# A two-layer hybrid mixer on one core: S5's tables of the first layer issued ahead of its first modulation, and the low parts of the out-projection's weights all on VectorE

## The chip, the core and the metric

The kernel runs on one core of one Trainium2 chip. The metric is the device time of one execution in microseconds (us); a run's figure is the median of several executions. Engines are named as the profile names them: PE is TensorE's matmuls and PEld its weight loads, DVE is VectorE, ACT is ScalarE, POOL is GpSimd, and SP is SyncE, whose queue issues most of the DMAs. Instructions of one engine run in the order in which they stand in its stream; what is late holds up what stands behind it.

## The reference, cut to what matters

Two layers run over 1280 tokens: 256 of a context and 1024 of the sequence, each with 1024 channels. A layer normalises its input and modulates it with values computed from a conditioning vector, projects it into four branches (RWKV-7, S5, SSD, GLA), mixes in each branch along the tokens, and projects the joined result back.

```python
def mixer_layer(h, mod, p, grid, init, need_out):
    shift, scale, gate = jnp.split(mod, 3, axis=-1)
    hn = rmsnorm(h, p['norm_pre']) * (1.0 + scale) + shift
    proj = hn @ p['w_in']
    ...
    y = jnp.concatenate([y_rw, y_s5, y_ssd, y_gla], axis=-1).astype(h.dtype) @ p['w_out']
    return h + gate * rmsnorm(y, p['norm_post']), states
```

The modulation is `mod = silu(c) @ ada_w[l] + ada_b[l]`. The S5 branch is a linear recurrence with complex diagonal coefficients. They come from parameters alone: `lam_bar = exp(lam * dt)`, `b_bar = ((lam_bar - 1) / lam) * b`. Nothing in them depends on the input or on the modulation.

## The kernel before

**Arithmetic.** Big products are made in three passes with 32-bit numbers that are split in a high part (rounded to the type fp32r) and a low part (the remainder): high by high, low by high, high by low. So weights and inputs are split on the chip. `split` (L1543) loads a half tile of 128x512 into one of two stage buffers, copies it to the high part on ScalarE (L1551) and subtracts it to make the low part; the engine of that subtraction is its last argument, VectorE unless it says "p" for GpSimd. All two-operand elementwise instructions pass through the helper `tt` at L342, and all matmuls through L330, so rows are told apart by their tiles.

**Order.** The program is written down layer by layer, and a scheduler then orders the instructions of each engine: among those which it finds ready by its own model of time, the one written first goes first. Tiles come from pools with a fixed number of buffers, and an instruction which needs a buffer waits until one is free. Pool T (L296) has eight buffers of 1280 columns, H (L302) six.

**Start of the first layer**, in `project` (L1714). `load_par` and `ada_in` load the parameters and the conditioning vector. `ada(0, 0)` (L1468) makes shift and scale in four pieces; each takes eight weight loads of 256 KB through a ring of four buffers (tile i_o), matmuls into a pj bank, copies on ScalarE and VectorE (L1488), and two small sums into the tile md. `prenorm` (L1500) takes five blocks of 256 columns: two loads into T buffers (n_x), squares on ScalarE, sums of squares on TensorE, an inverse root by eleven small VectorE instructions (qnx, qny, qnt), the product with it on VectorE and GpSimd, the modulation on VectorE and ScalarE, the cast to hi (L1528) and the subtraction to lo, of which one half is on each of VectorE and GpSimd. The last step needs md of all pieces. After that `load_con(False)` loads constants, and the projections start with the tiles misc and gk; their weights have four buffers, so that TensorE gets no others until the input's last block has passed through these two.

**S5's tables**, `s5_prep` (L705). Two parameter loads go into T buffers; three T buffers (all called z) are held to the end of the step. A setup of many small VectorE instructions makes powers and phases. Then each of four quarters makes complex products, the real half on VectorE and the imaginary half on GpSimd (z_w, z_o, z_es, z_ec, with z_tm), transposes and multiplies on TensorE in the one PSUM tile pz, and stores the tables to DRAM from SP (L828, L878, L880); their H buffers come free when the stores have landed. `s5_quarter` reads the tables much later, in the RWKV stage. The tuple MO gives the order in which a layer writes down its steps: p is `s5_prep`, g the GLA branch, s the SSD branch, r RWKV's projections. Before the change, p comes first in both layers, behind the projections of misc and gk.

**The out-projection**, `out_proj` (L1647). It splits eight weight tiles o_w0 to o_w7 of two halves each; the low parts alternate between GpSimd (even tiles) and VectorE (odd tiles). Then it goes over blocks of 256 columns. For the first block TensorE takes the weight tiles as they come. Just ahead of it stands the end of the RWKV stage, whose last steps make r_yt on VectorE and GpSimd and store it from GpSimd's queue (yd, L1454).

Of the kernel before, what the change touches and what calls it, by code (L numbers as in the profile page):

```python
# [24 lines left out]
KD = D // 128  # L25
# [205 lines left out]
ORDER = (3, 2, 4, 1, 0)  # L231
SJ = (3,5,6,7,9,10,11)

MO = 'pgsr'

RL = ('sm rq re', 'sm re rq')
RLL = 'rl hp tp qp'
# [20 lines left out]
class K:  # L258
# [1388 lines left out]
    def out_proj(self, l, h, dst, hi=None, lo=None):  # L1647
# [3 lines left out]
                          **{n: "oy" for n in ("o_yh", "o_yl", "o_y")}, **{n: "oo" for n in ("o_o", "o_acc", "o_sq", "o_x")})  # L1651
        W = []
        for m in range(8):
            W.append([x.rearrange("p (k m) -> p k m", k=KD) for x in self.split("o_w", f"o_w{m}", [128, 1024], 1, self.A["wout"][l, m], "pv"[m % 2])])
        nb = 1 if hi else 2
        for b in (0, 2, 3, 1, 4) if hi else (2, 3, 1, 4):
            b0 = b * 256
# [8 lines left out]
            x = self.R("o_x", [128, KD, 256])  # L1666
# [47 lines left out]
    def project(self, l, hi, lo, h):  # L1714

        outs = l == 0
        t0 = 0 if outs else TC
        self.l, self.fd, self.lates = l, {}, []
        self.rm = self.dr.tile([10, 128, 12, 128], F32, name=f"rm{l}")
        with ExitStack() as es:  # L1720
            if l == 0:
                self.pools(es, NT_, NQ_, NH_, left=AL[0].split(), **PA)
            else:
                self.pools(es, NT_, NQ_, NH_, right=AL[1].split(), **PA)
            if l == 0:
                self.load_par(0)
                self.ada_in()
                for _ in self.ada(0, 0, "pj", ("i_o", 4)):
                    pass
                self.prenorm(h, hi, lo)  # L1730
                self.load_par(1)
                pieces = self.adas(0)
            else:
                pieces = iter(())
            self.load_con(False)
            small = self.S("omu", [128, 10])
            self.omu, self.kkh = small[:, 0:8], small[:, 8:10]
            self.ts(self.omu, self.p("mu", 0, 8), -1.0, 1.0, OP.mult, OP.add)
            self.ts(self.kkh, self.p("kk", 0, 2), 0.5, None, OP.mult, OP.bypass)

            def gla():
                if G1[l] == "misc gk":
                    self.proj("gq", hi, lo, t0)
                self.proj_tok("gv", hi, lo)
                self.proj_tok("gg", hi, lo, t0 // 128)
                self.gla(Lazy(self, t0), outs)

            def ssd():
                for n in ("sB", "sC", "sx0", "sx1"):
                    self.proj(n, hi, lo)  # L1750
                self.proj_tok("sz", hi, lo, t0 // 128)
                self.ssd(Lazy(self, t0), outs)

            def rw():
                for n in ("k0", "k1", "wl", "al", "r0", "r1", "v0", "v1"):
                    self.rw_proj(n, hi, lo, outs)
                    next(pieces, None)

            self.proj(G1[l], hi, lo, t0)
            for n in MO:  # L1760
                {"p": lambda: self.s5_prep(l), "g": gla, "s": ssd, "r": rw}[n]()
            for _ in pieces:
                pass
# [63 lines left out]
```

## Time and profile before

| what | us |
|---|---|
| median of 3 runs | 2244.4 |
| lowest and highest of them | 2242.67, 2246.63 |
| the profiled execution, its own time | 2243.13 |
| its span, first to last instruction | 2241.4 |
| PE, DVE, ACT, POOL busy in it | 1947.4, 1529.2, 916.7, 846.5 |

The profile is of one execution. "Busy" is the time in which an engine had an instruction of the kind in work; a matmul's end is modelled. A row of a timeline gives start, duration, engine, line, operation, what is written and read, and in brackets the engine's idle time just before it and what ended it.

### The profile page before, as it was taken

How to read it: one execution, taken by the hardware profiler on the slowest of the kernel's cores; microseconds unless marked ns; L12 is line 12 of the kernel's file. 1: busy time of each engine (PE TensorE's matmuls, PEld its weight loads, DVE VectorE, ACT ScalarE, POOL GpSimd, SP SyncE). 2: the span in 40 equal slices, each digit the busy share in tenths (PEclk: the TensorE clock that was granted, in tenths of full speed). 3: DMA queues.
4: the chain of work that ended last, by engine and by line, in shares of the span. 5: the costliest groups of instructions: out<-in, count | busy, mean ns of one | idle time of the engine just before them, and what ended most of it. 6: DMA issues, size and time to landing. Idle time of an engine off the chain costs nothing. (4 is left out here: it accounts for less than half of the span.)

```text
span 2241.4 us, 45148 instructions
## 1 busy us (share of the span) xinstructions
PE 1947.4 (87%) x17712; PEld 1664.7 (74%) x17712; DVE 1529.2 (68%) x3423; ACT 916.7 (41%) x2009; POOL 846.5 (38%) x965
## 2 busy tenths in 40 slices
PE   6777999999997887878799779999999787889697
PEld 4667889678886676765799667887888676676497
DVE  3877646794146888885377786677754899896344
ACT  2434314333256447632233544234335755544220
POOL 0446460342024455532322255522332454542222
PEclk9889999999998888979999899999999989889698
DMA  7234425434633222214333335242234232212332
GB/s 247 74 118 132 157 83 170 128 115 133 187 99 116 88 74 81 70 40 140 90 114 113 120 125 175 89 145 80 70 112 125 98 105 68 86 47 73 122 104 95
DMA packets 204021, 246.83 MB, mean 110 GB/s; under 512 B 28384, under 2 KB 145632, under 8 KB 203808
## 3 DMA queue, kind: packets, MB, share of 16 engines
q1 hardware_dynamic: 169936, 213.13, 30.6%
q10 hardware_dynamic: 33008, 28.45, 3.9%
q8 instruction: 139, 2.28, 0.4%
q0 software_dynamic: 864, 2.36, 0.3%
q14 instruction: 74, 0.61, 0.1%
HBM read 169.27 MB, written 76.71 MB: 110 GB/s over the span
## 5 line engine op out<-in xcount | busy, mean ns | idle before, releaser
L330 PE MATMUL pj<-hi,i_wh 128*128 128x512 f32 (+1 forms) x696 | 180.2, 379 | 18.3 <-DVE hi L1528 13.2
L330 PE MATMUL pj<-lo,i_wh 128*128 128x512 f32 (+1 forms) x696 | 176.9, 372 | 0.1
L330 PE MATMUL pj<-hi,i_wl 128*128 128x512 f32 (+1 forms) x696 | 174.3, 368 | 2.7 <-DVE i_wl L342 2.7
L342 DVE TENSOR_TENSOR i_wl<-i_w,i_wh 128x512 fp32r<-128x512 f32 x108 | 84.8, 791 | 107.6 <-ACT i_wh L1551 37.6
L330 PEld LDWEIGHTS pj<-hi,i_wh 128*128 128x128 f32 x696 | 124.2, 199 | 43.1 <-DVE hi L1528 13.4
L330 PEld LDWEIGHTS pj<-hi,i_wl 128*128 128x128 f32 x696 | 123.9, 195 | 25.6 <-DVE i_wl L342 3.2
L330 PEld LDWEIGHTS pj<-lo,i_wh 128*128 128x128 f32 x696 | 124.0, 197 | 22.6 <-issue 2.6
L330 PE MATMUL px<-r_UV,r_A 128*64 128x64 f32 x1216 | 108.2, 247 | 17.0 <-DVE r_UV L1379 9.8
L330 PEld LDWEIGHTS px<-r_UV,r_A 128*64 128x64 f32 x1216 | 92.6, 157 | 37.5 <-DVE r_UV L1379 13.9
L1551 ACT CAST i_wh<-i_w 128x512 fp32r<-128x512 f32 x108 | 66.0, 620 | 122.0 <-PE pj L330 80.8
L1289 DVE TENSOR_TENSOR r_X<-r_X,r_tp 128x30 f32<-128x30 f32 (+1 forms) x300 | 93.8, 313 | 8.0
L342 DVE TENSOR_TENSOR r_tp<-r_N,r_X 128x30 f32<-128x30 f32 (+1 forms) x300 | 90.5, 302 | 7.2
L330 PE MATMUL pb<-r_AD,r_BK 128*128 128x256 f32 x320 | 85.2, 407 | 5.5 <-POOL r_BK L342 3.6
L342 POOL TENSOR_TENSOR r_S<-r_S,r_PM 64x256 f32<-64x256 f32 x72 | 54.0, 750 | 79.0 <-DVE r_S L342 66.8
L342 DVE TENSOR_TENSOR r_A<-pb,rcon 128x512 f32<-128x512 f32 x80 | 53.5, 682 | 42.2 <-PE pb L330 41.9
L330 PEld LDWEIGHTS pb<-r_AD,r_BK 128*128 128x128 f32 x320 | 60.9, 201 | 17.1 <-POOL r_BK L342 3.9
L330 PE MATMUL pj<-i_wh,hi 128*128 128x256 f32 x448 | 71.0, 296 | 2.9 <-ACT i_wh L1551 1.5
L345 POOL TENSOR_SCALAR r_AD<-r_AR 64x512 f32<-64x512 f32 (+1 forms) x80 | 54.4, 680 | 48.9 <-PE pb L330 42.4
L330 PE MATMUL pu<-r_rs,r_TT 128*64 128x128 f32 x320 | 49.2, 303 | 21.1 <-ACT r_rs L1375 20.8
L342 POOL TENSOR_TENSOR o_o<-o_o,o_x 128x512 f32<-128x512 f32 x18 | 23.8, 1323 | 114.7 <-DVE o_o L348 113.5
L330 PE MATMUL pj<-i_wl,hi 128*128 128x256 f32 x448 | 66.8, 289 | 0.2 <-DVE i_wl L342 0.2
L330 PEld LDWEIGHTS pj<-i_wh,hi 128*128 128x128 f32 x448 | 61.4, 198 | 6.7 <-issue 2.7
(469 smaller groups left out, 5445.9 us busy)
## 6 DMA issues: line engine op xcount, KB each, us to landing
i_w<-in_win SPq DMA_DIRECT2D x108, 256.0 KB, 3.0
r_in<-rm SPq DMA_DIRECT2D x36, 512.0 KB, 4.5
a_w<-in_ada SPq DMA_DIRECT2D x64, 256.0 KB, 3.8
rm<-i_o SPq DMA_DIRECT2D x48, 256.0 KB, 2.5
o_y<-yd SPq DMA_DIRECT2D x36, 256.0 KB, 3.0
i_o<-in_ada SPq DMA_DIRECT2D x32, 256.0 KB, 4.6
z_st<-s5t SPq DMA_DIRECT2D x32, 256.0 KB, 2.7
o_w<-in_wout SPq DMA_DIRECT2D x32, 256.0 KB, 2.7
```

The source lines that it names most:

```text
L330: self.nc.tensor.matmul(out, lhsT, rhs, start=start, stop=stop, skip_group_check=True)
L342: (self.nc.vector if e == "v" else self.nc.gpsimd).tensor_tensor(out, a, b, op)
L345: (self.nc.vector if e == "v" else self.nc.gpsimd).tensor_scalar(out, a, s1, s2, op0, op1)
L1289: last = nc.vector.tensor_tensor(X[:, :, :i, r0:4], X[:, :, :i, r0:4], tmp[:, :, :i, r0:], OP.add)
L1551: self.nc.scalar.copy(hi[:, v], w)
```

## The change

`s5_prep` of the first layer, and `load_con(False)`, whose constants it uses, are written down ahead of `ada(0, 0)`; the second layer keeps its order. In `out_proj` the last argument of `split` is dropped, so that all low parts of the weights are made on VectorE. Nothing else differs; no arithmetic is added or left out.

```diff
-MO = 'pgsr'
+MO = ('gsr', 'pgsr')
...
-            W.append([x.rearrange("p (k m) -> p k m", k=KD) for x in self.split("o_w", f"o_w{m}", [128, 1024], 1, self.A["wout"][l, m], "pv"[m % 2])])
+            W.append([x.rearrange("p (k m) -> p k m", k=KD) for x in self.split("o_w", f"o_w{m}", [128, 1024], 1, self.A["wout"][l, m])])
...
             if l == 0:
                 self.load_par(0)
                 self.ada_in()
+                self.load_con(False)
+                self.s5_prep(l)
                 for _ in self.ada(0, 0, "pj", ("i_o", 4)):
                     pass
                 self.prenorm(h, hi, lo)
...
-            self.load_con(False)
+            if l:
+                self.load_con(False)
...
-            for n in MO:
+            for n in MO[l]:
                 {"p": lambda: self.s5_prep(l), "g": gla, "s": ssd, "r": rw}[n]()
```

## Rows read from the trace of the kernel before

**Rows 1.** The page, parts 1 and 2: busy time by engine; TensorE in 40 slices.

```profile
PE 1947.4 (87%) x17712; PEld 1664.7 (74%) x17712; DVE 1529.2 (68%) x3423; ACT 916.7 (41%) x2009; POOL 846.5 (38%) x965
...
PE   6777999999997887878799779999999787889697
```

**Rows 2.** Stretches: busy us (count) of PE, PEld, DVE, ACT, POOL; clock, DMA, GB/s.

```profile
0.00:74.50 74.50, 52.01 (x408) 38.38 (x409) 29.97 (x112) 24.94 (x51) 8.15 (x11) 1.00 0.69 220
74.50:130.00 55.50, 36.76 (x176) 30.52 (x174) 54.22 (x155) 17.60 (x35) 28.20 (x17) 0.75 0.11 38
130.00:250.00 120.00, 103.94 (x875) 93.62 (x875) 85.27 (x102) 57.45 (x102) 70.17 (x45) 0.94 0.45 148
250.00:400.00 150.00, 150.00 (x1502) 129.23 (x1492) 88.93 (x164) 46.81 (x102) 52.48 (x79) 0.99 0.41 130
```

**Rows 3.** Timeline, VectorE and GpSimd: start, duration, line, operation; last md, last lo.

```profile
74.57 0.15 DVE L348 SCALAR_TENSOR_TENSOR md<-md,par 128x4 f32<-128x4 f32 x1
...
125.57 2.53 POOL L342 TENSOR_TENSOR lo<-n_x,hi 128x1024 fp32r<-128x1024 f32 x1 [11.18 <-DVE hi L1528]
```

**Rows 4.** Instructions by tile, the tables': least, median, greatest ns; first and last start.

```profile
L342 DVE TENSOR_TENSOR z<-z x160: 109/176/2479, 68.5 to 1299.8; 128x16 f32<-128x16 f32 x96, 128x32 f32<-128x32 f32 x24, 128x64 f32<-128x64 f32 x24, 128x256 f32<-128x256 f32 x8
...
L342 POOL TENSOR_TENSOR z_w<-z x8: 1062/1426/2676, 91.5 to 1379.7; 128x512 f32<-128x512 f32 x8
L342 DVE TENSOR_TENSOR z_w<-z x8: 671/689/2041, 92.9 to 1380.5; 128x512 f32<-128x512 f32 x8
...
L342 POOL TENSOR_TENSOR z_es<-z x8: 1684/1741/2713, 136.4 to 1399.7; 128x640 f32<-128x640 f32 x8
```

**Rows 5.** Instructions by tile, the prenorm's.

```profile
L1528 DVE CAST hi<-n_x x10: 678/680/687, 47.9 to 124.8; 128x1024 fp32r<-128x1024 f32 x10
...
L342 DVE TENSOR_TENSOR lo<-n_x,hi x5: 1212/1216/1226, 49.2 to 123.5; 128x1024 fp32r<-128x1024 f32 x5
```

**Rows 6.** Timeline of VectorE and GpSimd: small operation alone, and beside lo.

```profile
32.78 0.16 DVE L342 TENSOR_TENSOR qnt<-qny 128x2 f32<-128x2 f32 x1
...
77.35 2.35 DVE L342 TENSOR_TENSOR qnt<-qny 128x2 f32<-128x2 f32 x1
...
76.97 8.15 POOL L342 TENSOR_TENSOR lo<-n_x,hi 128x1024 fp32r<-128x1024 f32 x3 [11.61 <-DVE hi L1528]
```

**Rows 7.** Timeline of GpSimd, second layer: first z_w, last z_es.

```profile
1271.37 1.89 POOL L342 TENSOR_TENSOR z_w<-z 128x512 f32<-128x512 f32 x1 [31.79 <-DVE z L342]
...
1405.45 2.03 POOL L342 TENSOR_TENSOR z_es<-z_es,z_tm 128x640 f32<-128x640 f32 x1
```

**Rows 8.** Waits of the SP queue, 75 to 250 us, then 0 to 75 us.

```profile
SPq L828 <- ACT z_wt L842: 33.9, 5, 26.6
...
SPq L828 <- DVE z_bp L857: 2.6, 1, 2.6
...
SPq L1482 <- PE pj L330: 20.7, 18, 6.4
```

**Rows 9.** Stretch 130 to 250 us, instructions on the tables' PSUM tile pz alone.

```profile
130.00:250.00 120.00, 10.52 (x208) 7.54 (x208) 3.55 (x16) 11.78 (x38) 0.94 0.45 148
```

**Rows 10.** Timelines of the first layer's end of RWKV: ScalarE, VectorE, GpSimd.

```profile
1051.96 1.14 ACT L1551 CAST o_w0h<-o_w 128x512 fp32r<-128x512 f32 x2
...
1067.73 0.88 DVE L348 SCALAR_TENSOR_TENSOR r_yt<-r_yt,par,r_ks 128x256 f32<-128x256 f32 x2
...
1068.74 1.26 POOL L342 TENSOR_TENSOR r_yt<-r_yt,r_fin 128x512 f32<-128x512 f32 x1 [8.09 <-DVE r_yt L348]
...
1071.79 2.50 POOL L342 TENSOR_TENSOR o_w0l<-o_w,o_w0h 128x512 fp32r<-128x512 f32 x2
```

**Rows 11.** Timeline of GpSimd, the second layer's.

```profile
2112.00 2.50 POOL L342 TENSOR_TENSOR o_w0l<-o_w,o_w0h 128x512 fp32r<-128x512 f32 x2
```

**Rows 12.** Instructions by tile, stage o_w.

```profile
L342 POOL TENSOR_TENSOR o_w2l<-o_w,o_w2h x4: 1277/1282/1291, 1080.4 to 2127.5; 128x512 fp32r<-128x512 f32 x4
L342 DVE TENSOR_TENSOR o_w3l<-o_w,o_w3h x4: 691/692/694, 1084.9 to 2132.4; 128x512 fp32r<-128x512 f32 x4
```

## The prediction

> **What bounds the kernel now.** I read the page first: TensorE is busy 87% of the span, and its line of 40 slices is 9 in long stretches and 6 to 8 at the start and in others [rows 1]. Where it says 9, only less matmul work could help; where it does not, TensorE waits, and a change can only shorten such waits. So I cut the first 400 us into stretches at two events [rows 2]: the last modulation value of the first layer (md, written at 74.57 us) and the last low part of the normed input (lo, ending at 128.1 us, called P below) [rows 3]. Up to 74.5 us TensorE waits for ada's weights, and VectorE is idle for 44.5 us of it. From there to P VectorE is busy 54.2 of 55.5 us: it is the bound, TensorE works 36.8 us at a granted clock of 0.75, between its two levels of 1.2 and 2.4 GHz. From 130 to 250 us TensorE leaves out 16 us at 0.94, and from 250 to 400 us it is full. Hence the S5 tables share VectorE with the prenorm before P, and disturb TensorE's feed until 250 us.
>
> **What the tables cost.** In the first layer they are 211 VectorE and 40 GpSimd instructions, of whose groups [rows 4] show the largest (counts there are for both layers). By the least durations, a quarter has on VectorE three z_w and three z_o at 0.67 us, three operations on 640 elements at 0.8 to 1.3 us and eleven small ones, about 9.1 us; on GpSimd six at 1.06 and 1.29 us and three at 1.6 to 1.7 us, 11.8 us. Four quarters: 83.6 us. The setup before them is some 130 VectorE instructions, mostly at 0.18 us, about 27 us with the larger ones. For the prenorm's five blocks of 256 columns and what else ran, summed in the same way over the instructions (lo at 1.21 us on VectorE and 2.5 us on GpSimd, the casts of hi at 0.68 us [rows 5]), about 34 us lie ahead of 74.5 us and 37 us behind.
>
> The two engines disturb each other: a 128x2 operation takes 0.16 us alone and 2.35 us while GpSimd runs the three lo subtractions [rows 6]. Between 74.5 us and P work of 68 us by least durations (37 prenorm, 31 tables) was done in 55.5 us, so the pair does **1.23 us of work in 1 us**. The Trainium skill, SBUF — State Buffer, section Who interferes with whom, says that this port pair is an exclusive lock for a VectorE instruction with two SBUF inputs against GpSimd's reads; the rows agree for the operation shown, not for all, since 1.23 is over 1. By that rule alone the tables' halves on the two engines would never overlap; this is the second rival below, with the rate 1.0.
>
> **Part 1, the tables ahead of ada.** The order is made by priority, so the tables now go first on every engine where they are ready.
> - Setup: the parameters land some 5 us into the run. 27 us of setup plus about 12 us of prenorm work on VectorE fill it until about 40 us; this was idle time, so it costs nothing. If ada's small copies and sums wait behind it, a few tenths each.
> - Quarters: in the second layer, where the tables stand ahead of nearly everything, GpSimd's first z_w starts at 1271.4 us and the last z_es ends at 1407.5 us [rows 7]: 34 us a quarter, longer than their 20.9 us of work, for they wait on buffers and stores. Starting at 35 us they end at about 171 us.
> - Ada: two more loads for constants and two for parameters stand ahead of its weights on SP, about 2 us, and I take 78 us for its end. Its later loads stand behind the tables' stores on SP, 70 issues a layer in all. SP waited in that way for 97 us between 75 and 250 us in eight groups, the longest shown, of which 26.6 us were one wait; the rest is 17.7 us a quarter. SP already waits 20.7 us for ada's ring in the first 75 us [rows 8]; the 1.25 quarters until 78 us bring 22 us, which I put beside it at no cost. If that cover is gone, ada is late: the third rival.
> - P: from 78 us the tables take 20.9/34 = 0.61 us per us of the pair's 1.23, the prenorm gets 0.62, and its 37 us take 60 us: 138 us. The tables hold three of the eight buffers in which the input is loaded, so its last blocks come about one block later; I add 5 us. **P moves from 128 to 143 us**, the wrong way. At rate 1.0 it would be 168 us (after ada the tables leave 0.39), at the 1.4 that I get from the same sum between 90 and 110 us, 130 us.
> - After P: from 130 to 250 us TensorE was busy 103.9 us, of which 10.5 us were the tables' own matmuls and transposes [rows 2, 9]. The other 93.4 us are 88 us at full clock. At P = 143 us 0.8 of a quarter is left, 17 us of work where 76 us were, so I keep 16 x 17/76 = 3.6 us of TensorE's idle time and 3 us for the rest. 143 + 88 + 6.6 = 238 us stands against 250 us: **12 us gained**. The bounds are P = 130 us, 24 us gained, and P = 168 us, where nothing of the tables is left: 168 + 88 = 256 us, 6 us lost.
> - The tables' activations and their three table loads on ScalarE, busy 25 of the first 74.5 us, cost nothing there. Their stores meet ada's loads, but the queues were busy 0.69 of that stretch and 0.11 of the next [rows 2]. Past 250 us TensorE is full, so what is gained by then should stay; that the GLA branch gets its buffers earlier is counted as nothing.
>
> **Part 2, the low parts on VectorE.** At the end of the first layer's RWKV part, ScalarE had the high part of the first weight tile at 1053.1 us, but GpSimd's subtraction runs at 1071.8 us: it stands in order behind the last r_yt and two DMA issues. VectorE is through with r_yt at 1068.6 us [rows 10]. The second layer shows the same, 2112.0 us [rows 11] with r_yt's sums ending 3.2 us earlier. Until then both stage buffers are full, and no further weight loads start. On VectorE the start comes 3.2 us earlier, the first tile is ready 0.6 us sooner (0.69 against 1.28 us [rows 12]), and three more even tiles save 0.6 us each in the chain of load, cast, subtraction: 3.2 + 0.6 + 1.8 = 5.6 us a layer, **11 us in all**, as TensorE waits for each tile in its first block and has the other blocks' work afterwards. VectorE takes on 16 subtractions in all, 11 us, in stretches where it waits for casts. Bounds: 1.5 us a layer, if TensorE can fill the gaps with the next block's tiles or SP is held by the loads of y; 18.7 us a layer, if the subtraction is put into VectorE's earlier gaps. I take 5.6 because GpSimd, idle before its last r_yt, did not get it there either.
>
> **The sum.** The profiled execution took 2243.1 us (span 2241.4 us), 1.3 us under the median of 2244.4 us. 2243.1 - 12 - 11 = 2220 us, and on the median's level **2221 us**.
>
> **The rivals.**
> 1. *The quarters fit.* If stores and buffers do not hold the quarters up while GpSimd is free, three are done by ada's end. With P at 130 us part 1 gives 24 us, and with part 2 up to 15 us: 2205 us. For it: GpSimd is busy only 8.15 us up to 74.5 us [rows 2]. Against: the 34 us a quarter.
> 2. *The two engines shut each other out.* P is 168 us, part 1 loses 6 us, part 2 gives 11 us: 2239 us. For it: the 2.35 us row. Against: the rate of 1.23.
> 3. *Ada's loads stand behind the stores on SP: slower.* If the 17.7 us a quarter fall on ada in full over 2.5 quarters, its end goes from 78 to 122 us. The prenorm then has 49 us beside the last quarters (30 us of work), 6 us alone, and its input, in five buffers, comes late as well, 6 us: P = 183 us, 183 + 88 = 271 us, 21 us lost. With 11 us from part 2 it is 10 us slower: 2254 us. It decides from an ada end of about 116 us. For it: one queue, in order, and the 26.6 us wait. Against: while the tables wait, ada's ready loads are meant to be put ahead of them.
> 4. *Little moves:* the order puts the tables where they were, or takes back later what is gained; 0 to 11 us from part 2 remain, 2240 us.
>
> **How the numbers follow.** About 0.2% (4.5 us) is what a measurement of this kernel can tell from no change. The forecast has 42%, rival 1 22%, rival 2 14% (half of it faster by more than that), rival 3 13%, rival 4 9% (5% of it faster). Faster: 42 + 22 + 7 + 5 = 76%; the same: 7 + 4 = 11%; slower: 13%. The range goes from 2196 us (rival 1 with the early subtraction in one layer) to 2250 us (rival 3 with P 4 us earlier).
>
> **What would show it.** The tables' setup must end near 40 us and their last store near 170 us; ada's last md should stand near 78 us, and P between 135 and 155 us; from P on TensorE should be at 9 tenths or more, and its full stretch begin some 12 us earlier relative to its work. In the out-projection, o_w0l must follow r_yt on VectorE at once, and the first block end 5 to 6 us sooner after it. An md later than 110 us, or P later than 175 us, makes the forecast wrong; so does a gain that is given back between 400 and 700 us, where VectorE is the busier engine.

## The result: 18 us slower, and the profile after

The changed kernel takes 2263.5 us (median of 6 runs, 2257.7 to 2268.5) against 2245.5 us for the kernel before on the same chip: a ratio of 1.0075, 95% interval 1.0057 to 1.0092. I had forecast 2221 us, and 2196 to 2250 us for the range. The sign was wrong.

The profiled execution of the changed kernel took 2268.5 us, with a span of 2266.7 us against 2241.4 us. It is the slowest of its six and the profile before is near the fastest, so the profiles lie 25.3 us apart where the medians lie 18.0. Read beside [rows 1], the slices of TensorE's busy share and clock, of the changed kernel, already show two places:

```profile
PE 1965.5 (87%) x17712; PEld 1683.7 (74%) x17712; DVE 1524.9 (67%) x3439; ACT 916.4 (40%) x2007; POOL 829.1 (37%) x949
...
PE   5689999999998877888799779989999777778697
...
PEclk8589999999997898888999889989999788889698
```

The first two slices are lower than before, and so are four of the five from the 33rd to the 37th (57 us each). The others differ by a digit or two here and there. To put sizes on this I took the same instruction in both traces as a milestone:

| milestone | before, us | after, us | difference |
|---|---|---|---|
| ada's last md of layer 0, end | 74.7 | 102.9 | +28.2 |
| last lo of the prenorm (P), end | 128.1 | 150.7 | +22.6 |
| a fifth of all projection matmuls done | 241.1 | 245.7 | +4.6 |
| RWKV stage of layer 0, first pu | 706.1 | 709.0 | +2.9 |
| the same stage, last pu | 1049.0 | 1062.7 | +13.7 |
| out-projection of layer 0, last matmul | 1213.2 | 1225.5 | +12.3 |
| RWKV stage of layer 1, first pu | 1762.1 | 1772.9 | +10.8 |
| the same stage, last pu | 2080.9 | 2110.5 | +29.6 |
| out-projection of layer 1, last matmul | 2224.7 | 2250.0 | +25.3 |

Read the steps between the lines. The front, where part 1 was made, ends 3 us late, which is not clear of the spread: in the seven kernels of this study that leave the front as it was, the first pu stands between 704.4 and 709.4 us. The two RWKV stages, which neither part edits, take 10.8 and 18.8 us longer. From the last pu to the last matmul of the out-projection, where part 2 was made, it takes 1.4 and 4.3 us less. Nearly all that was lost was lost where nothing was changed.

The front first: windows of the changed kernel (the columns of [rows 2]) and the timeline of md and of P, the answer to [rows 3].

```profile
0.00:74.50 74.50, 43.57 (x408) 32.62 (x410) 61.82 (x213) 27.29 (x59) 28.45 (x25) 0.79 0.69 217
74.50:130.00 55.50, 39.98 (x298) 32.95 (x288) 51.37 (x84) 20.08 (x50) 37.96 (x22) 0.70 0.41 129
130.00:250.00 120.00, 104.54 (x762) 92.06 (x761) 46.56 (x69) 48.94 (x76) 39.48 (x27) 0.91 0.41 138
250.00:400.00 150.00, 150.00 (x1476) 129.03 (x1474) 89.16 (x158) 45.26 (x93) 49.61 (x72) 0.99 0.34 108
```

```profile
102.73 0.16 DVE L348 SCALAR_TENSOR_TENSOR md<-md,par 128x4 f32<-128x4 f32 x1
...
148.22 2.51 POOL L342 TENSOR_TENSOR lo<-n_x,hi 128x1024 fp32r<-128x1024 f32 x1 [4.79 <-DVE hi L1528]
```

VectorE is filled from the start (61.8 us busy up to 74.5 us, where it had 30.0), as forecast, and GpSimd takes its share. But ada is 28 us late, and the granted clock of the first stretch falls from 1.00 to 0.79, between its two levels of 1.2 and 2.4 GHz, while TensorE, waiting more, is busy 43.6 us instead of 52.0.

The start of the out-projection in the changed kernel, the answer to [rows 10]:

```profile
1078.58 0.88 DVE L348 SCALAR_TENSOR_TENSOR r_yt<-r_yt,par,r_ks 128x256 f32<-128x256 f32 x2
1079.38 1.28 DVE L342 TENSOR_TENSOR o_w0l<-o_w,o_w0h 128x512 fp32r<-128x512 f32 x2
1079.59 2.21 POOL L342 TENSOR_TENSOR r_yt<-r_yt,r_fin 128x512 f32<-128x512 f32 x1 [7.27 <-DVE r_yt L348]
```

o_w0l now follows r_yt on VectorE at once, where it stood 3.2 us later on GpSimd.

Last the two RWKV stages as windows, from the first to the last pu (the matmul of the recurrent state), before and then after:

```profile
706.10:1049.00 342.90, 282.71 (x3473) 235.74 (x3472) 286.42 (x636) 179.74 (x431) 157.67 (x207) 0.88 0.27 82
1762.10:2080.90 318.80, 265.92 (x3364) 219.89 (x3364) 274.27 (x616) 173.07 (x420) 153.25 (x203) 0.91 0.26 80
```

```profile
709.00:1062.70 353.70, 289.88 (x3477) 240.10 (x3478) 283.72 (x636) 179.78 (x428) 164.54 (x207) 0.86 0.25 79
1772.90:2110.50 337.60, 271.00 (x3364) 227.69 (x3364) 271.83 (x615) 174.13 (x420) 151.40 (x203) 0.86 0.25 75
```

The numbers of instructions are the same (within a few at the edges of the windows), and VectorE and ScalarE work as long as before. What grew is TensorE's idle time (in layer 1 from 52.9 to 66.6 us) and, at a lower clock, its busy time. The same work, then, but in another order: on VectorE and ScalarE, the instructions of the two traces run in the same sequence for about two thirds of these stages in layer 0 and for a third in layer 1, while they agree to some 95% in the projections of the last 200 us ahead of the first stage. The program's planner writes the order down by its own estimate of when things are ready. That it had a different state to start from here is argued; the runs below show what a change of the order costs.

### The profile page after: what moved, and what is told of

It is laid out like the page before. It is cut to its first block, busy times and chain, and to the rows that moved or that the text cites. A ratio compares the mean times of both kernels' runs of the same rounds, so it can differ in the third digit from the quotient of the medians.

```text
span 2266.7 us, 45119 instructions
## 1 busy us (share of the span) xinstructions
PE 1965.5 (87%) x17712; PEld 1683.7 (74%) x17712; DVE 1524.9 (67%) x3439; ACT 916.4 (40%) x2007; POOL 829.1 (37%) x949
## 5 line engine op out<-in xcount | busy, mean ns | idle before, releaser
L342 DVE TENSOR_TENSOR i_wl<-i_w,i_wh 128x512 fp32r<-128x512 f32 x108 | 89.8, 836 | 153.2 <-PE pj L330 73.8
L330 PE MATMUL pb<-r_AD,r_BK 128*128 128x256 f32 x320 | 90.0, 426 | 4.6 <-POOL r_BK L342 2.1
L1289 DVE TENSOR_TENSOR r_X<-r_X,r_tp 128x30 f32<-128x30 f32 (+1 forms) x300 | 84.4, 281 | 7.6
L342 POOL TENSOR_TENSOR o_acc<-o_acc,o_sq 128x512 f32<-128x512 f32 x23 | 31.1, 1353 | 113.1 <-ACT o_sq L339 113.0
L330 PEld LDWEIGHTS pu<-r_rs,r_TT 128*64 128x64 f32 x320 | 41.6, 160 | 36.4 <-ACT r_rs L1375 32.7
L339 ACT ACTIVATE r_BK<-r_BK,r_PM 128x128 f32<-128x128 f32 x160 | 58.4, 396 | 21.8 <-PE pb L330 20.0
```

The lines of the kernel that those rows point to most:

```text
L330: self.nc.tensor.matmul(out, lhsT, rhs, start=start, stop=stop, skip_group_check=True)
L339: self.nc.scalar.activation(out=out, in_=in_, func=f, **kw)
L342: (self.nc.vector if e == "v" else self.nc.gpsimd).tensor_tensor(out, a, b, op)
L1289: last = nc.vector.tensor_tensor(X[:, :, :i, r0:4], X[:, :, :i, r0:4], tmp[:, :, :i, r0:], OP.add)
```

## The experiments

Two theories, and rivals. **A**: an edit anywhere makes the planner order the RWKV stages anew, and the order sets their length; the edits' own price is small. **B**: part 1's lateness at the front is handed down. **C**: part 2 overloads VectorE. **D**: the changed front leaves TensorE with a lower clock. All times are medians, each with its ratio to the kernel before on the same chip; the stages are from one profiled execution. Stage lengths are from first to last pu.

### The parts alone, and two controls

Part 1 alone (p1_tables) leaves out the second hunk of the change, part 2 alone (p2_lows) is that hunk only. The controls add one line to the kernel before, at its very start:

```
 null_v:
+        nc.vector.memset(self.cp.tile([128, 64], F32, name="nul"), 0.0)
 null_p:
+        nc.gpsimd.memset(self.cp.tile([128, 32], F32, name="nul"), 0.0)
```

> The tables ahead of ada alone; the out-projection's low parts as before (odd ones on GpSimd). Theory A (order): the front costs little, and the time is lost where an unedited stage gets another order. Then the last md of ada stands near 101 us and P near 151 us as in the changed kernel, the RWKV stage of layer 0 starts some 3 us late (before: 706 us) and gets 8 to 11 us longer than 343 us, the projections of layer 1 keep their length, and the RWKV stage of layer 1 (before: 319 us) comes out anywhere from 10 us shorter to 20 us longer, since its order differs from both kernels'. Rival B (own price): the late md and P are handed down, all of the +18 us of the changed kernel are there by 706 us, and part 1 alone is +18 to +25 us with both RWKV stages at their old lengths (within 3 us).

> The low parts of the out-projection's weights on VectorE alone; the tables where they were. Theory A (order): everything up to the end of the RWKV stage of layer 0 is as before within 1 us (1068.6 us for its last r_yt on VectorE); o_w0l starts 3 us earlier in both layers, the out-projections end 0 to 6 us earlier after it; the RWKV stage of layer 1, which has another order, changes its length by 3 us or more either way though nothing in it was edited. In sum -10 to +10 us. Rival C (VectorE overloaded): the 11 us of subtractions delay VectorE's chain in the out-projection, whose length grows by 3 us or more in each layer, with the RWKV stages unchanged.

> A control: the kernel before with one memset of an unused tile of 128x64 on VectorE at its very start, some 0.1 us of work, and nothing else. Theory A (order): the order of the instructions that the program's planner writes down reacts to so small a shift; one or both RWKV stages change length by 3 us or more, and the time leaves that of the kernel before by more than 0.2%, either way. Rivals B and C: the time stays within 0.2% and both stages keep their length within 2 us.

> A second control: the kernel before with one memset of an unused tile of 128x32 on GpSimd at its very start. Theory A: as in the first control, an RWKV stage changes by 3 us or more and the time by over 0.2%, not necessarily with the same sign as there; together with the first control and the two parts this gives the spread that an order alone makes. Rivals B and C: within 0.2%, stages within 2 us.

| kernel | time, us | ratio (95%) | stage of layer 0 | stage of layer 1 |
|---|---|---|---|---|
| p1_tables | 2284.4 | 1.0166 (1.0140 to 1.0191) | 355.1 | 344.2 |
| p2_lows | 2246.1 | 0.9994 (0.9978 to 1.0011) | 343.2 | 325.0 |
| null_v | 2245.5 | 0.9994 (0.9975 to 1.0012) | 341.2 | 326.7 |
| null_p | 2252.3 | 1.0022 (1.0002 to 1.0041) | 343.0 | 319.1 |

(Of the low parts it is the even ones that GpSimd makes before the change; the expectations of p1_tables and p1_late say odd.) Part 1 alone is slower than both parts together, by 21 us of medians. Its front is that of the changed kernel within 1.5 us, and the first pu of layer 0 stands at 708.9 us, 2.8 us late; so B, which wanted the whole loss there by 706 us, falls. Both stages are longer, as A expects, though both by more than its ranges (12 us where 8 to 11 stood, and 25 where up to 20 stood). Part 2 changes nothing in sum. The out-projections gain; the stage of layer 1, whose order it changes, took 325.0 us, 6 us more than before, but that lies within the spread of the controls below. Two later kernels with this same order, al_qp and a_q, took 328.0 and 326.9 us. Against C, no out-projection got longer: from VectorE's last r_yt to the last matmul they take 143.4 and 112.0 us, where it was 144.6 and 115.9.

The controls did not do what they were made for: the order of VectorE and ScalarE in their traces is that of before throughout, so the planner did not react, and the 0.2% of null_p, at the edge of its interval, are no effect of an order. So A's first half, that an edit anywhere makes a new order, is false as it stands. They tell something else: with one and the same order, the profiled stage of layer 1 comes out between 318.8 and 326.7 us, and that of layer 0 between 341.2 and 343.0 us. This is how far single executions lie apart.

### An order changed alone

If the order is the cause, it must be enough to change it in the kernel before. Memsets of a tile that is zero anyway, ahead of the RWKV stage, move the planner's estimate by a little. The first three edits and a fourth, of another kind:

```
 b_l1v2 (before), b_l0v12 (before), a_l0v12 (changed kernel), at the start of the RWKV part:
-        nc.gpsimd.memset(self.zero, 0.0)
+        nc.gpsimd.memset(self.zero, 0.0); [nc.vector.memset(self.zero, 0.0) for _ in range(2 if not outs else 0)]
 (b_l0v12 and a_l0v12: range(12 if outs else 0))
 a_late (changed kernel):
                 self.load_con(False)
-                self.s5_prep(l)
                 for _ in self.ada(0, 0, "pj", ("i_o", 4)):
                     pass
+                self.s5_prep(l)
                 self.prenorm(h, hi, lo)
```

> The kernel before with two memsets on VectorE (r_z, set to zero once more) at the start of the RWKV part of layer 1, well under 1 us of work, and neither part of the change. They tip the planner: the order of VectorE's and ScalarE's instructions in the RWKV stage of layer 1 becomes that of part 1 alone, instruction for instruction, while all before it stays as it was. Theory A (order): everything up to the first pu of layer 1 (1762 us) is as before, the stage from first to last pu takes about 344 us as in part 1 alone instead of 319 to 327, and the time rises by 17 to 25 us, to 2263 to 2271 us. Rivals B (own price of the edits, handed down) and D (a lower clock that the changed front leaves behind): nothing changed ahead, so the stage stays at 319 to 327 us and the time within 5 us of before.

> The kernel before with twelve such memsets on VectorE at the start of the RWKV part of layer 0, some 2 us of work, neither part of the change. The order in the RWKV stage of layer 0 becomes that of the changed kernel (98% of VectorE's and ScalarE's instructions in the same order), that of layer 1 becomes part 1's in full. Theory A: first to last pu of layer 0 353 to 357 us instead of 341 to 343, of layer 1 340 to 346 us instead of 319 to 327; with the memsets' 2 us the time is 2270 to 2285 us, part 1's own loss without part 1. Rivals B and D: at most the memsets' 2 us, 2246 to 2250 us.

> The changed kernel with the same twelve memsets at the start of the RWKV part of layer 0. Its order there stays nearly as it was (98%), but that of layer 1 becomes that of the kernel before, instruction for instruction. Theory A: the RWKV stage of layer 0 keeps its 354 to 356 us, that of layer 1 goes from 338 us back to 319 to 327; the time falls by 10 to 17 us, to 2246 to 2253 us. Rivals B and D: layer 1 keeps its 338 us, and the time goes up by the memsets' 2 us to about 2265 us.

> The changed kernel with the tables' call behind ada's first part instead of ahead of it, and still ahead of the prenorm; part 2 as in the change. In both RWKV stages the order is that of the kernel before, instruction for instruction. Theory A: first to last pu 341 to 345 us in layer 0, 319 to 327 in layer 1; ada's md is back near 75 us, P between 145 and 170 us, the start of the RWKV stage of layer 0 within 6 us of 706; with part 2's 1 and 4 us the time comes out at 2236 to 2250 us. Rival B: tables beside the prenorm cost the same or more, 2262 us or later, already there at the start of the RWKV stage of layer 0. Rival D: the stages stay near 354 and 338 us whatever their order, as long as the front is changed.

| kernel | time, us | ratio (95%) | stage of layer 0 | stage of layer 1 |
|---|---|---|---|---|
| b_l1v2 | 2273.1 | 1.0120 (1.0095 to 1.0146) | 341.8 | 340.5 |
| b_l0v12 | 2249.0 | 1.0008 (0.9993 to 1.0023) | 340.5 | 323.5 |
| a_l0v12 | 2267.3 | 1.0093 (1.0075 to 1.0111) | 355.2 | 336.9 |
| a_late | 2225.0 | 0.9895 (0.9861 to 0.9928) | 339.7 | 320.6 |

**b_l1v2** is the decisive one. It contains neither part of the change, and its milestones stand within 2.1 us of before's up to the end of layer 0's out-projection. Two memsets make it 25 us slower: 14 to 22 in the RWKV stage of layer 1, against the controls' 318.8 to 326.7 us, and some 5 in the projections ahead of it, where the order changed in places too (450 us from the out-projection's end to their own, where it was 443 to 446 in the order of before). Its expectation had the stage right (about 344 us), but not these 5 us, and the time lies 2 us above its range. TensorE's longest waits in that stage (total us, times, longest), of the kernel before:

```profile
PE pu L330 <- ACT r_rs L1375: 10.7, 8, 3.1
PE p L330 <- DVE z_x L342: 7.3, 3, 3.4
PE pi L330 <- ACT r_Rb L1324: 4.5, 5, 1.3
```

The stage's window in b_l1v2, and then the same waits there:

```profile
1770.30:2110.80 340.50, 275.83 (x3364) 229.78 (x3364) 275.77 (x615) 173.41 (x418) 153.64 (x203) 0.85 0.24 74
```

```profile
PE pu L330 <- ACT r_rs L1375: 25.1, 12, 6.2
PE p L330 <- DMA z_st<-s5t: 4.2, 2, 2.9
PE px L330 <- DVE r_UV L1379: 4.1, 2, 3.4
PE pi L330 <- DVE r_DN L1309: 4.1, 2, 3.0
```

The counts are the same, 3364 matmuls each, and VectorE's work is 274.3 and 275.8 us. But in the new order the state's matmul pu waits 25.1 us for ScalarE's r_rs, where it waited 10.7 us, and the waits on r_UV and r_DN are longer (1.2 and 0.8 us before). Here is the longest wait, of 6.2 us, in rows of VectorE, ScalarE and TensorE:

```profile
1819.59 0.41 DVE L1374 COPY r_rs<-px 64x256 f32<-64x256 f32 x1
1817.57 0.63 ACT L339 ACTIVATE r_th<-ps,r_sc 128x128 f32<-128x128 f32 x2 [3.71 <-POOL r_ks L345]
1821.17 0.63 ACT L339 ACTIVATE r_a<-ps,r_sc 128x128 f32<-128x128 f32 x2 [2.98 <-POOL r_BK L342]
1821.83 0.36 ACT L1375 COPY r_rs<-px 64x256 f32<-64x256 f32 x1
1822.24 1.12 PE L330 MATMUL pu<-r_rs,r_TT 128*64 128x128 f32 x4 [6.23 <-ACT r_rs L1375]
```

VectorE copied its half of the same px at 1819.6 us, so px was ready by then. ScalarE's half stands behind r_a, for which ScalarE sat idle 3.0 us until GpSimd had finished r_BK.

TensorE's idle time in the stage goes from 52.9 to 64.7 us, its granted clock from 0.91 to 0.85, and so its busy time from 265.9 to 275.8 us. Against the one profile of before, the loss is about half waiting and half clock; the waiting is the firmer half, as null_v, in the order of before, was busy 275.7 us too. Since the front is that of before, D falls as a cause.

The Trainium skill, PSUM — Partial Sum Buffer, section Engine vs sequencer instructions, states that the queues of ScalarE, VectorE and GpSimd are strictly first in, first out. The rows agree with it: ScalarE did not take up its half of r_rs while r_a, ahead of it, waited.

The changed kernel has another order in this stage, and its waits there are spread wider. Its wait for r_rs is 15.0 us (13.7 in a_l0v12, which has the same order), where the five kernels with the order of before have 10.7 to 14.8 us; what it adds stands in the other rows:

```profile
PE pu L330 <- ACT r_rs L1375: 15.0, 8, 6.0
PE ps L330 <- ACT r_a L339: 6.8, 3, 3.1
PE pi L330 <- DVE r_X L1289: 5.5, 1, 5.5
PE pi L330 <- DVE r_DN L1309: 5.4, 3, 3.7
PE px L330 <- DVE r_UV L1379: 5.1, 3, 3.6
```

So the 25 us on r_rs are how part 1's order costs its time (22.6 to 25.1 us in four kernels), not how the change's own order does.

**b_l0v12 and a_l0v12** ran in another order than their expectations say. In the traces b_l0v12 has the order of before and a_l0v12 that of the changed kernel, instruction for instruction. So they became controls with twelve memsets more: same order, same time within 4 us, and the same stages. What they were to show is shown by a later run.

**a_late** has both parts, and in the RWKV stages the order of before: in full in layer 1, and in layer 0 for all but the last twentieth on VectorE. It takes 2225.0 us, 23 us less than before and 38 less than the changed kernel, with stages of 339.7 and 320.6 us. This is 11 us less than A's range, because the first stage begins 11.9 us earlier than before, though ada's md is at 83.3 us and not back near 75. So the tables ahead of the prenorm and the low parts on VectorE are worth having; it is the place of one call that decided. Of the 43.3 us between the two spans (2266.7 and 2223.4 us) the front makes 14.8, and the two stages, in their other order, 14.0 and 17.0.

### Layer 0's order, the stores' queues, and part 2's worth

```
 b_l0v3i4 (before), in the loop of the RWKV part over i:
+                _ = [nc.vector.memset(self.zero, 0.0) for _ in range(3 if outs and i == 4 else 0)]
 al_qp (a_late) and a_q (changed kernel), at the tables' three kinds of stores:
-                nc.sync.dma_start(...)
+                (nc.sync if l else nc.gpsimd).dma_start(...)        (al_qp; in a_q nc.scalar)
 p1_late: a_late without part 2
```

> The kernel before with three memsets on VectorE (r_z set to zero again) ahead of the fifth step of layer 0's RWKV loop, under 1 us of work, neither part of the change. This time the order written down was compared afresh: up to layer 0's RWKV stage it is that of before, in that stage 97% of VectorE's and ScalarE's instructions stand as in the changed kernel, in layer 1's 91%. Theory A (order): first pu of layer 0 at 706 us within 3, then first to last pu 352 to 357 us instead of 340 to 343; in layer 1 333 to 344 us instead of 319 to 327; the time 2266 to 2280 us, the changed kernel's loss without either part. Rivals B (own price of the edits) and D (a changed front leaves a lower clock): both stages at their old lengths, 2243 to 2252 us.

> The kernel with the tables' call behind ada, and besides the tables' stores of layer 0 issued by GpSimd's queue instead of SP's. The order in layer 0's RWKV stage is the changed kernel's again (98%), in layer 1's that of part 2 alone. Theory A: the quick front is kept or improved (ada's md at 74 to 78 us, since no store stands ahead of its loads on SP; first pu of layer 0 between 688 and 700 us), but the stage after it takes 352 to 357 us, that of layer 1 322 to 328 us; 2234 to 2248 us in all. Rival D: with the quick front the stages stay at 340 and 320 us, 2218 to 2228 us.

> The changed kernel with the tables' stores of layer 0 issued by ScalarE's queue instead of SP's; the tables stay ahead of ada. If the late md comes from ada's loads standing behind waiting stores on SP, it moves from 103 us to 75 to 85 us, P from 151 to 130 to 145 us, and the first pu of layer 0 from 709 to 690 to 702 us. If it comes from VectorE, TensorE's bank or GpSimd serving the tables first, md stays at 98 to 105 us and P at 147 to 155 us. The RWKV stage of layer 0 has an order of its own here (half as in either kernel), so no length is expected for it; that of layer 1 has part 2's own order, 322 to 328 us.

> The kernel with the tables' call behind ada, without part 2: odd low parts of the out-projection's weights on GpSimd again. Layer 0's RWKV stage has the order of before, layer 1's an order of its own (55% as before). If part 2 is worth what the pairs so far show, from VectorE's last r_yt to the last matmul of the out-projection it takes 144 to 147 us in layer 0 and 115 to 117 us in layer 1, against 142 and 113 with part 2; up to the last r_yt of layer 0 all stands as with part 2 within 2 us (1054 us). If part 2 is worth the 5.6 us a layer that were forecast, the out-projections are 148 and 118 us. The RWKV stage of layer 1 comes out between 319 and 345 us by its order; no total is expected beyond 2227 to 2255 us.

| kernel | time, us | ratio (95%) | md / P | first pu, layer 0 | stages |
|---|---|---|---|---|---|
| b_l0v3i4 | 2269.3 | 1.0096 (1.0073 to 1.0119) | 76.2 / 129.6 | 709.4 | 354.1, 336.0 |
| al_qp | 2265.9 | 1.0085 (1.0068 to 1.0103) | 89.5 / 153.3 | 716.3 | 354.3, 328.0 |
| a_q | 2249.7 | 1.0008 (0.9996 to 1.0021) | 98.9 / 149.2 | 711.8 | 340.8, 326.9 |
| p1_late | 2239.7 | 0.9969 (0.9956 to 0.9982) | 84.4 / 145.6 | 693.7 | 337.5, 333.5 |

**b_l0v3i4** reproduces the changed kernel's whole loss without either of its parts, 23 us by medians, with the front of before (P at 129.6 us). Its windows:

```profile
709.40:1063.50 354.10, 291.31 (x3465) 240.08 (x3465) 283.07 (x632) 180.72 (x432) 161.10 (x207) 0.86 0.26 77
1778.90:2114.90 336.00, 277.02 (x3364) 232.89 (x3364) 271.93 (x615) 173.72 (x420) 150.75 (x203) 0.85 0.25 76
```

They have the changed kernel's lengths again, within 2 us, with its order in 92 to 98% of layer 0's stage and some 90% of layer 1's. In layer 0 more of the loss is busy time than idle time: idle 62.8 us against 60.2 before, busy 291.3 against 282.7 us at 0.86 instead of 0.88. The five kernels with this order in layer 0 all ran the stage at 0.86, the kernels with the order of before at 0.87 to 0.90.

**al_qp** missed at the front. The stores on GpSimd's queue made md and P later by 6 and 9 us, not earlier. GpSimd issues a store in 0.58 us and waits in order for its data, up to 8.7 us for one store, and the prenorm's and tables' work stands behind. That the one caused the other is argued. Its stage of layer 0 has the changed kernel's order (96% on VectorE) and length (354.3 us) although the tables stand behind ada, which is A's expectation; by the late front the time is 18 us above A's range.

**a_q** took the second branch of its expectation: off SP, the stores let md come 4 us earlier, not 18 to 28, and P hardly moved. Its stage of layer 0 has an order of its own, half of it as before, and yet took 340.8 us: a new order need not be a longer one. **p1_late** gave 146.5 us in layer 0, as its first branch had it, and 118.2 in layer 1, the figure of its other branch, so a single pair does not decide; I take part 2's worth from all kernels of this study. From the last r_yt on VectorE to the last matmul of the out-projection it takes 144.6 to 148.4 us in layer 0 without part 2 (mean of 8 kernels 146.6) and 142.2 to 146.0 with it (9 kernels, 144.3); in layer 1 114.0 to 118.2 (mean 115.7) and 112.0 to 113.8 (112.6). The ranges overlap in layer 0; the means differ by 2.3 and 3.2 us.

### What held ada up, and an order behind the quick front

```
 al_l1v2: a_late with b_l1v2's two memsets
 a_cp (changed kernel), a_q_cp (a_q):
-                (nc.vector.tensor_copy if q % 2 else nc.scalar.copy)(...)
+                (nc.vector.tensor_copy if q % 2 and (l or part) else nc.scalar.copy)(...)
```

> The kernel with the tables' call behind ada and part 2 (2225 us), plus two memsets of r_z on VectorE at the start of the RWKV part of layer 1. The order in layer 0's RWKV stage stays that of before, in layer 1's it becomes part 1's in full. Theory A (order): up to layer 1's projections as without the memsets within 3 us, layer 1's stage from first to last pu 339 to 346 us instead of 320; the time 2240 to 2252 us, the gain all but gone. Rival D (front): 2222 to 2229 us.

> The changed kernel (tables ahead of ada, stores on SP) with the eight copies of ada's first part in layer 0 that VectorE makes given to ScalarE. If what holds ada up is VectorE, which serves the tables first, its md moves from 103 us to 80 to 92 us and P from 151 to 140 to 147 us. If it is SP's stores alone, md stays at 99 to 105 us. The RWKV stage of layer 0 has an order of its own (59% as in either kernel), that of layer 1 part 1's: 340 to 346 us.

> Both at once: the stores of layer 0's tables on ScalarE's queue and ada's copies on ScalarE. If the two hold ada up in turn, md comes to 75 to 85 us; if the tables' share of TensorE and GpSimd or the md sums on VectorE also count, it stays above 88 us. P follows md at 44 to 62 us' distance. Orders of its own in both RWKV stages.

| kernel | time, us | ratio (95%) | md / P | first pu, layer 0 | stages |
|---|---|---|---|---|---|
| al_l1v2 | 2251.2 | 1.0011 (0.9997 to 1.0025) | 85.1 / 146.0 | 691.4 | 338.4, 344.3 |
| a_cp | 2261.9 | 1.0068 (1.0056 to 1.0081) | 90.2 / 150.8 | 705.9 | 346.4, 340.6 |
| a_q_cp | 2259.9 | 1.0049 (1.0036 to 1.0062) | 79.8 / 155.8 | 713.4 | 347.4, 333.3 |

**al_l1v2** turns a kernel that is 1% faster into one that is the same as before, by two memsets. Here is its stage of layer 1, to be held against a_late's:

```profile
1749.30:2093.60 344.30, 280.43 (x3364) 232.50 (x3364) 276.30 (x615) 173.56 (x419) 153.39 (x203) 0.83 0.24 74
```

```profile
1746.30:2066.90 320.60, 267.55 (x3362) 220.82 (x3364) 275.66 (x616) 173.00 (x420) 152.04 (x203) 0.90 0.26 80
```

**a_cp and a_q_cp** show what held ada up: VectorE, whose copies of ada's sums stood behind the tables' work, for 13 us; VectorE and SP together for 23 of the 28. SP's stores alone were worth 4 us (a_q), and 10 us once the copies were gone from VectorE. But P did not follow, against both expectations. With md at 79.8 us it came at 155.8 us, later than with md at 102.9. So ada does not set P. That the whole of VectorE's and GpSimd's work ahead of it does is argued: up to P, VectorE is busy 129.7 of 150.7 us in the changed kernel and 131.1 of 155.8 in a_q_cp.

Fourteen kernels share the order of layer 1's stage on VectorE and ScalarE with others. Sorted by it, the profiled stages fall into groups:

| order of layer 1's stage | kernels | length, us | idle, us | clock |
|---|---|---|---|---|
| before's | before, null_v, null_p, b_l0v12, a_late | 318.8 to 326.7 | 51.0 to 54.6 | 0.87 to 0.91 |
| part 2's | p2_lows, al_qp, a_q | 325.0 to 328.0 | 54.1 to 59.2 | 0.87 to 0.89 |
| the change's | after, a_l0v12 | 336.9, 337.6 | 62.5, 66.6 | 0.85, 0.86 |
| part 1's | p1_tables, b_l1v2, al_l1v2, a_cp | 340.5 to 344.3 | 60.8 to 64.7 | 0.83 to 0.85 |

In three of the groups kernels with different fronts stand side by side. Between the first group and the last, idle time and busy time grow by about 10 us each in the mean.

## Why the prediction was wrong, by its own steps

**The step that failed is one sentence: "Past 250 us TensorE is full, so what is gained by then should stay".** It priced an edit at the front and one at the ends, and left what lies between as it was. The chain of waits was thought through, the list of instructions not: I knew that the order comes from a planner and used it for the tables, but not for the stages behind. The RWKV stages' new orders cost 10.8 and 18.8 us, 29.6 together; with the front's 2.9 and the 7.2 us that out-projections and layer 1's projections gained, this is the 25.3 us between the spans. The forecast had 23 us the other way. Of the 48 us between the two, the stages are 29.6, the front 14.9 (12 gained in the forecast, 2.9 lost), and the out-projections 5.3; layer 1's projections gave back 1.5. Rival 4 had an order that "takes back later what is gained", down to no gain, and its 9%; that it could take more than that had no chance and no price.

**Part 1.** VectorE's idle start was filled, as forecast. The tables' last store went out at 171.9 us, where 171 stood, but partly by luck: the first z_w on GpSimd started at 20.0 us, where 35 stood, the quarters took 35.5 us each where 34 stood, and the last store went out behind eight others, some 10 us after the last product. The tables had 13 us of work left when P came, where 17 stood. P was 150.7 us, inside 130 to 168 but 8 us behind the 143 taken.
- Ada at 78 us: it was 102.9. VectorE's copies for ada, ordered behind ready work of the tables, cost 13 us of it; the prediction gave them "a few tenths each". SP's waits, put beside the ring "at no cost", were worth 4 to 10 us. Rival 3 named SP alone for this and had P follow ada; neither held, so its sign, slower, came true by another path.
- From P on I had 94.6 us to the work that the kernel before had done by 250 us. It took 104.0 us (150.7 to 254.7). TensorE's idle time was 5.4 us, near the 6.6 taken, and its busy time 98.6 us where I had 88. I had taken all of the tables' 10.5 us off and scaled the rest to full clock. The window of the changed kernel for the first 47 us after P shows 0.93 of the clock; TensorE's waits there show one of 4.3 us for a load; and SP's timeline shows that load behind the tables' last stores:

```profile
150.70:197.80 47.10, 42.83 (x282) 36.77 (x281) 15.30 (x20) 19.91 (x35) 10.59 (x6) 0.93 0.43 141
```

```profile
PE ps L330 <- DMA l_misc<-f_misc: 4.3, 1, 4.3
```

```profile
166.88 4.94 SPq L880 DMA_DIRECT2D s5m<-s5k x8
171.92 0.53 SPq L828 DMA_DIRECT2D s5t<-z_es x1
172.49 0.43 SPq L1644 DMA_DIRECT2D l_misc<-f_misc x1
```

  So instead of 12 us gained, 4.7 us were lost at 250 us, and 2.9 at the first RWKV stage. With the tables behind ada (a_late) md was 83.3 and P 144.3 us, and the same stage began 11.9 us earlier: there, the forecast's P and its gain of 12 us came out, in a kernel for which it was not made. Up to the same matmul, with a tenth of all projections done, it took 39.5 us after P, TensorE without a gap at a clock of 1.00; there the load of l_misc stood ahead of the tables' last stores:

```profile
144.30:183.80 39.50, 39.50 (x290) 35.08 (x289) 19.32 (x30) 19.94 (x35) 14.15 (x9) 1.00 0.63 202
```

- Rival 2, the rate of 1.0, put P at 168 us. Its own terms give more: 37 us of work at 0.39 from 78 us end near 172 us, and with the same 5 us for the buffers that is 177 us. No run put P later than 155.8 us. An estimate for the changed kernel, summed by the least durations of each group as in the forecast, is 84 us of work on the two engines in the 72.7 us from 78 us to P, 1.16 us in 1 us: the overlap was there, if less than the 1.23. The Trainium skill, SBUF — State Buffer, section Who interferes with whom, calls the shared port pair an exclusive lock; the sum over mixed work does not go by that alone.

**Part 2.** The mechanism was right: the subtraction starts as r_yt ends on VectorE instead of 3.2 us later, in each layer. The size was off: 5.4 us in all instead of 11, 2.3 and 3.2 us a layer against 5.6, inside its bounds of 1.5 to 18.7. That is about the earlier start alone; of the 0.6 and 1.8 us that I added for quicker tiles nothing is seen. C, that VectorE would be overloaded there, was not seen in any pair.

**The signs in the text** were partly of use. "An md later than 110 us" did not come, and P stayed under 175 us. "A gain given back between 400 and 700 us" looked at the wrong place: between a fifth of the projections and the first RWKV stage nothing was lost (4.6 to 2.9 us).

**What stays open.** Why the planner's estimate prefers an order that is 20 us longer on the chip was not tried. Nor is it told apart whether a late r_rs first costs waiting and the clock follows, or the reverse; the rows show both together. In the change's own orders the added waits are spread over many producers, and which instruction out of place costs most was not tried.

## What to carry to other kernels

Where a planner writes the order by estimated times, compare the order of the unedited stages before pricing an edit: here two idle memsets moved the time by 1.2%, more than the whole change is worth with the orders unchanged. Judge an edit by the stage that it touches, with the other stages in the same order, and try it at a second place in the program before it is given up: the same two parts are 0.75% slower with the tables' call ahead of ada and 1.05% faster behind it. A producer that has become later is only worth repairing if its consumer waits for it and not for another engine: md moved by 23 us, and P did not come sooner.

## What the runs showed that I had not expected

- More idle time in the RWKV stage came with a lower granted clock, and with more busy time for the same matmuls. In layer 1 the clock was 0.87 to 0.91 in the five kernels with the order of before, with 51 to 55 us of idle time, and 0.83 to 0.85 in the four with part 1's order, with 61 to 65 us. Idle time alone does not set it: null_v, in the order of before and with 51 us, ran the stage at 0.87, a_late with 53 us at 0.90.
- With the order unchanged, single executions of one kernel lie up to 0.8% apart (2238.5 to 2256.4 us in 29 runs of the kernel before on one chip), and the length of one stage, with one order in five kernels, by 8 us. The orders of the change and of part 1 cost more than that in layer 1, but a single profile of each kernel would not have told the controls from part 2.
